# One expert pair leaves the DRAM path: units 4 to 12 instead of 4 to 13 return through accumulating DMAs, unit 13 through one-hot matmuls

## The chip, the cores and the metric

The kernel runs on one core of a Trainium2 chip. The metric is the time of one execution in microseconds (us) as the device gives it; the time before is the median of three runs.

## What is computed

Two transformer blocks follow each other over 512 tokens of width 1024, in float32. Each block is a mixer (attention of one kind beside a recurrence of another), an output projection onto the residual h, and a mixture of experts. The change is in the mixture of the first block:

```python
for e in range(N_EXPERTS):                      # 32 experts, two chosen per token
    h = jax.nn.silu(x2d @ w_gate[e]) * (x2d @ w_up[e])      # 1024 -> 256
    y = y + combine[:, e:e + 1] * (h @ w_down[e])           # 256 -> 1024
h = h + y
```

`combine` is zero but for the two experts that a router chose for the token, so only the rows that an expert has been given are computed. After it comes a norm and the second block.

## The kernel before, in words

**Units.** The 32 experts of the first mixture are worked off in 16 units of two. A unit has 128 lanes, 64 for each expert of the pair; an expert with more than 64 tokens would need a further round, which is a loop over `body` (L1589) whose count is read from memory and is zero for these inputs, so the loop is skipped by a branch on every engine. For each unit u: POOL gathers the rows by an indirect DMA into `xg` (two units ahead), TensorE transposes them (L1609), multiplies with the gate and up weights of both experts (L1711, 64 instructions), ScalarE and VectorE make `hh` (L1714, L1715), TensorE transposes it (L1765, ScalarE copies it to `hT`, L1766), and one unit later the down product is made (L1655, 16 instructions).

**Weights.** Six loads of 1 MB for each unit (gate, up and down of two experts) are issued from SP (L1540) in a fixed order through a ring of buffers: gate and up of u, then down of u - 1, but for the last unit down of 14 first, then gate and up of 15, then its down.

**Return of the rows.** The rows of a unit must be multiplied by their weight and added into the residual h at their tokens. There are two ways.
- One-hot products (`down`, `scatter`): ScalarE and VectorE split the product into a high and a low part (L1785, L1786), VectorE makes a matrix `SC` of ones and zeros from the lanes' token numbers (L1790), and for each of 4 token tiles n and 2 halves d TensorE multiplies `SC` with both parts (L1806, L1807) into a PSUM bank; VectorE adds the bank into `h[:, n]` (L1800). Two banks, `ch` and `pq`, take turns. Units 0 to 3 go this way, two units at a time, and units 14 and 15 together after the skipped loop, in `end`.
- By DRAM (`by_dram`): ScalarE scales the product (L1664), POOL writes its rows by an indirect DMA to a DRAM buffer `yd` (L1665). When the last such unit has written, eight indirect DMAs (L1730), for choice c = 0, 1 and token tile n = 0 to 3, fetch each token's row from `yd` and add it to `h[:, n]` while they write it. A token whose expert isn't among these units has an index out of bounds, and its row is left out. Units 4 to 13 (experts 8 to 27) go this way. `yd` is cleared once, much earlier, in the first mixer (L503).

Which units go by DRAM is set by `FROM` and `BYDRAM` at the top; `far` (L1681) is their range, and the accumulating DMAs stand in the text at `u == far[-1] + 1`, after that step's `by_dram`.

**Order.** Between the engines a framework sets all waits from what the instructions read and write, so a VectorE add into `h[:, n]` waits for the accumulating DMAs into it, and the second accumulate into a tile for the first. The order on each engine is planned ahead from modelled costs: mostly the text's order, but an instruction whose inputs the plan has ready is pulled ahead of one that it has waiting. On the chip each engine then works strictly in that order. All engines pass the skipped loop together. Behind it `end` is written in a fixed order.

Of the kernel before, what the change touches and what calls it, by code (L numbers as in the profile page):

```python
# [25 lines left out]
SILU = "silu_and_others"  # L26

FROM = {1: 8, 2: 0}
BYDRAM = {1: 20, 2: 14}
CAP = {1: 64, 2: 96}  # L30
ZROW = {k: BYDRAM[k] * CAP[k] for k in CAP}
KAPPA = float(np.exp(-0.5))
# [37 lines left out]
def host_consts(inp):  # L70
    pc = {part: np.zeros((128, n), np.float32) for part, n in LAY.n.items()}

    def put(name, a):
        part, o, w = LAY.at[name]
        pc[part][:, o:o + w] = a
# [26 lines left out]
    for k, e in (1, np.arange(32)), (2, np.arange(16)):  # L102
        put("row%d" % k, one * np.where((e >= FROM[k]) & (e < FROM[k] + BYDRAM[k]), CAP[k] * (e - FROM[k]), 1e5))
    put("out1", i[:, None] + 128 * np.arange(16) - CAP[1] * FROM[1])
# [78 lines left out]
class Kern:  # L183
# [1459 lines left out]
    def moe1(self):  # L1643
# [34 lines left out]
        def body(num, wts, idx, first):  # L1678

            ys, prev = [], None  # L1680
            far = range(FROM[1] // 2, (FROM[1] + BYDRAM[1]) // 2) if first else ()  # L1681
            for u in range(2):
# [6 lines left out]
            def down_args(u, hT, num, wts):  # L1689
                return hT, [self.moe_next(mo) for _ in range(2)], wts[:, u:u + 1], onehot(u, yp.tile([128, T], R32, name="SC", bufs=3))  # L1690

            onehot = lambda u, SC: self.onehot(SC, mo, num, u)
            for u in range(mo.U):
# [13 lines left out]
                for m in range(2):  # L1707
                    d = p[:, m * 256:m * 256 + 256]
# [25 lines left out]
                hT = gp.tile([128, 2, 128], F32, name="hT", bufs=1)  # L1734
                turned(hh, hT)
                prev = u, hT
            if not first:
                self.scatter(ys[12:15], 1)
                self.scatter(ys[14:15], 0)
                hT = gp.tile([128, 2, 128], F32, name="hT", bufs=1)  # L1740
                turned(hh, hT)
                return first, None, *down_args(mo.U - 1, hT, num, wts)
# [19 lines left out]
        def turned(hh, hT):  # L1762
            q = self.ps("tr")
            for k in range(2):
                nc.tensor.transpose(q[:, k * 128:(k + 1) * 128], hh[:, k * 128:(k + 1) * 128], self.ident)  # L1765
            nc.scalar.activation(hT, q[:, 0:256].rearrange("p (k t) -> p k t", k=2), AF.Copy)  # L1766

        def end(first, y14, *args):
# [6 lines left out]
            for n in (0, 2, 1, 3):  # L1775
                for d in range(2):
                    self.scatter(ys, d, [n], ("so", "gu", "so", "dn"))

        self.moe_rounds(mo, body, None, end)
        self.sums_two([self.place(mo, 1) for _ in range(NT)], self.place(mo, 1))  # L1780
        mo.cr.close()
# [44 lines left out]
    def moe2(self, out):  # L1826
        nc, tc, mo = self.nc, self.tc, self.mo
        with mo.cx, mo.cr:
# [48 lines left out]
            def body(num, wts, idx, first):  # L1877
# [7 lines left out]
                for u in range(mo.U):  # L1885
# [37 lines left out]
                    if prev and not last:  # L1923
                        y = down(*prev, num, wts, not first or prev[0] >= BYDRAM[2], turned)
                    else:
# [114 lines left out]
```

## Time and profile before

| what | us |
|---|---|
| median of three runs | 1420.56 (1418.53 to 1422.75) |
| the profiled execution's own time | 1419.69 |
| its span, first to last instruction | 1417.9 |
| TensorE busy in the span | 1289.0 (91%) |
| VectorE, ScalarE, POOL busy | 841.6, 701.6, 410.2 |
| moved by DMA | 283.93 MB, mean 200 GB/s |

A span is cut into stretches, and each stretch has its own limit. In a row of the table of stretches the busy times of the engines stand beside the stretch's length, and the DMA share is the mean busy share of the 16 DMA engines. In the timeline a row is the start, the duration, the engine, the line, and what is written from what; "x16" is sixteen instructions in a row, and the bracket is the idle time before and what ended it. The first mixture's last units lie between about 640 and 723 us.

### The profile page before, as it was taken

The page shows a single profiled execution, that of the slowest core. Times are in us where ns is not written, and L with a number is a line of the kernel's source. Part 1 is how long each engine was busy: PE and PEld are TensorE (multiplying, and loading weights), DVE is VectorE, ACT ScalarE, POOL GpSimd, SP SyncE. Part 2 cuts the span into 40 slices and gives each one's busy share as a digit, 9 for nine tenths or more (in the row PEclk, how much of TensorE's full clock was granted, in tenths as well). Part 3 has the DMA queues.
Part 4 walks back from the last instruction along what each step waited for, and adds up shares of the span by engine and source line. Part 5 has one row for each costly group of instructions (what it writes and reads, how often), then busy time and mean ns, then how long its engine had stood idle before and what let it go on. Part 6 is the DMA issues. An engine that isn't in the chain of part 4 may idle for free.

```text
span 1417.9 us, 20482 instructions
## 1 busy us (share of the span) xinstructions
PE 1289.0 (91%) x7792; PEld 927.7 (65%) x7792; DVE 841.6 (59%) x1432; ACT 701.6 (49%) x1217; POOL 410.2 (29%) x329
## 2 busy tenths in 40 slices
PE   7999999999897999999379999999996999999993
PEld 5777766767696555554156776777894666666662
DVE  4679866566656131000075656657637799998895
ACT  6433433334634221211064555555545788888883
POOL 1000224241104101110366102011124555555445
PEclk9999999999998899999789999999997999999996
DMA  5232440000484999999832121202386999889943
GB/s 189 75 89 75 107 109 2 1 1 2 188 330 170 386 419 419 418 418 422 223 101 75 30 76 45 86 24 100 105 334 209 321 360 382 320 332 391 385 166 125
DMA packets 54452, 283.93 MB, mean 200 GB/s; under 512 B 8849, under 2 KB 9745, under 8 KB 28738
## 3 DMA queue, kind: packets, MB, share of 16 engines
q1 hardware_dynamic: 43634, 254.75, 47.9%
q0 software_dynamic: 9840, 26.39, 5.8%
q8 instruction: 66, 1.08, 0.3%
q10 hardware_dynamic: 864, 1.31, 0.3%
q14 instruction: 48, 0.39, 0.1%
HBM read 270.70 MB, written 22.29 MB: 207 GB/s over the span
## 4 chain that ended last, share of the span: by engine, by line
PE 68%; DVE 13%; DMA 11%; ACT 3%; issue 2%; POOL 1%; SPq 0%; DVEq 0%; POOLq 0%; ACTq 0%
PE mm L322 12%; PE ua L1903 4%; PE ua L1901 4%; PE ua L1902 4%; PE mm L1711 4%; DMA ew<-in_e1down_dram 3%; DMA ew<-in_e1up_dram 3%; PE ua L1655 2%; PE sb L322 2%; PE sb L1844 2%; PE sb L1843 2%; PE sb L1845 2%; PE sb L715 2%; DMA ew<-in_e1gate_dram 2%; DVE elo L1625 2%
## 5 line engine op out<-in xcount | busy, mean ns | idle before, releaser
L1625 DVE TENSOR_TENSOR elo<-ew,ehi 128x1024 fp32r<-128x1024 f32 x147 | 231.1, 1614 | 32.9 <-ACT ehi L1624 22.6
L1624 ACT ACTIVATE ehi<-ew 128x1024 fp32r<-128x1024 f32 x192 | 203.0, 1061 | 62.7 <-PE ua L1902 37.2
L322 PE MATMUL mm<-xh,whi 128*128 128x512 f32 (+1 forms) x384 | 155.9, 406 | 4.0 <-DVE hq L1143 3.7
L322 PE MATMUL mm<-xl,whi 128*128 128x512 f32 (+1 forms) x384 | 154.0, 401 | 0.5 <-DVE xl L354 0.3
L322 PE MATMUL mm<-xh,wlo 128*128 128x512 f32 (+1 forms) x384 | 152.8, 398 | 0.0
L1625 POOL TENSOR_TENSOR elo<-ew,ehi 128x1024 fp32r<-128x1024 f32 x45 | 125.9, 2799 | 64.8 <-ACT ehi L1624 63.0
L1711 PE MATMUL mm<-ew,xTh 128*64 128x256 f32 x1024 | 119.2, 386 | 6.4 <-DMA ew<-in_e1up_dram 4.7
L1903 PE MATMUL ua<-elo,xTh 128*96 128x512 f32 x256 | 102.9, 402 | 8.5 <-DVE elo L1625 8.4
L1711 PEld LDWEIGHTS mm<-ew,xTh 128*64 128x64 f32 x1024 | 73.5, 139 | 47.5 <-DMA ew<-in_e1up_dram 6.4
L1715 DVE TENSOR_TENSOR hh<-hh,mm 128x256 f32<-128x256 f32 x16 | 6.7, 421 | 163.5 <-ACT hh L1714 163.5
L1901 PE MATMUL ua<-ehi,xTh 128*96 128x512 f32 x256 | 102.3, 399 | 0.7 <-ACT xTh L1613 0.6
L1902 PE MATMUL ua<-ehi,xTl 128*96 128x512 f32 x256 | 101.8, 398 | 0.0
L296 ACT ACTIVATE whi<-w 128x1024 fp32r<-128x1024 f32 x53 | 55.9, 1057 | 91.1 <-PE mm L322 72.5
L297 DVE TENSOR_TENSOR wlo<-w,whi 128x1024 fp32r<-128x1024 f32 x52 | 63.7, 1227 | 51.7 <-ACT whi L296 51.5
L1596 POOL DMA_INDIRECT xg<-xd,idx x32 | 36.7, 1147 | 196.2 <-PE sb L1609 123.7
L322 PEld LDWEIGHTS mm<-xh,whi 128*128 128x128 f32 x384 | 73.4, 191 | 23.2 <-DVE hq L1143 5.4
L322 PEld LDWEIGHTS mm<-xl,whi 128*128 128x128 f32 x384 | 73.7, 192 | 16.7 <-issue 3.5
L322 PEld LDWEIGHTS mm<-xh,wlo 128*128 128x128 f32 x384 | 73.6, 192 | 16.0 <-issue 2.2
L1655 PE MATMUL ua<-ew,hT 128*64 128x512 f32 x240 | 66.4, 600 | 1.2 <-ACT hT L1766 1.1
L1714 ACT ACTIVATE hh<-mm 128x256 f32<-128x256 f32 x16 | 6.1, 383 | 112.8 <-PE mm L1711 112.8
L1903 PEld LDWEIGHTS ua<-elo,xTh 128*96 128x96 f32 x256 | 41.9, 164 | 30.6 <-DVE elo L1625 11.2
L1167 POOL TENSOR_TENSOR hAT<-hAT,hmt 128x512 f32<-128x512 f32 x16 | 22.1, 1381 | 118.9 <-DVE hmt L1166 118.3
(640 smaller groups left out, 3028.0 us busy)
## 6 DMA issues: line engine op xcount, KB each, us to landing
ew<-in_e1up_dram SPq DMA_DIRECT2D x32, 1024.0 KB, 17.8
ew<-in_e2up_dram SPq DMA_DIRECT2D x32, 1024.0 KB, 8.3
ew<-in_e2gate_dram SPq DMA_DIRECT2D x32, 1024.0 KB, 9.2
ew<-in_e2down_dram SPq DMA_DIRECT2D x32, 1024.0 KB, 12.5
ew<-in_e1gate_dram SPq DMA_DIRECT2D x31, 1024.0 KB, 19.5
ew<-in_e1down_dram SPq DMA_DIRECT2D x30, 1024.0 KB, 20.6
w<-in_win_dram SPq DMA_DIRECT2D x53, 512.0 KB, 3.6
ew<-in_wout_dram SPq DMA_DIRECT2D x8, 1024.0 KB, 6.9
```

The costliest lines, as they stand in the source:

```text
L296: nc.scalar.activation(hi, s, AF.Copy)
L297: (eng or nc.vector).tensor_tensor(lo, s, hi, OP.subtract)
L322: mm = lambda w, x, start=False, stop=False: nc.tensor.matmul(p[:, s], w[:, k], x[:, k, s], start=start, stop=stop, skip_group_check=parts ...
L715: nc.tensor.matmul(po[d, 0:128], v[:, kb, d], wT[hh][:, kb * 128:(kb + 1) * 128], start=kb == 0, stop=kb == b)
L1596: return self.nc.gpsimd.indirect_dma_start(out=xg, out_offset=None, in_=mo.xd, in_offset=bass.IndirectOffsetOnAxis(ap=idx[:, u:u + 1], axi ...
L1624: self.hi = nc.scalar.activation(hi, s, AF.Copy)
L1625: self.lo = (nc.gpsimd if pool else nc.vector).tensor_tensor(lo, s, hi, OP.subtract)
L1655: nc.tensor.matmul(p[hs(a)], hT[:, k, hs(a)], w[a][:, k * 1024 + d * 512:k * 1024 + d * 512 + 512], start=k == 0, stop=k == 1)
L1711: nc.tensor.matmul(d[hs(a)], xT[:, k, hs(a)], w[2 * m + a][:, k * 256:k * 256 + 256], start=k == 0, stop=k == KD - 1)
L1901: nc.tensor.matmul(p, xh[:, kk], hi[:, s], start=kk == 0, stop=False)
L1902: nc.tensor.matmul(p, xl[:, kk], hi[:, s], start=False, stop=False)
L1903: nc.tensor.matmul(p, xh[:, kk], lo[:, s], start=False, stop=kk == KD - 1)
```

## The change

`BYDRAM[1]`, the number of experts that return by DRAM, goes from 20 to 18. So `far` is units 4 to 12, the eight accumulating DMAs are issued at u = 13, unit 13 takes the branch of `down` (one-hot matrix, high and low part) at u = 14, and `yd`, its clearing and the bounds shrink from 1280 to 1152 rows. After the loop over the units, when unit 15's gate and up products have been written down in the text and before its transpose, unit 13's rows are added by `scatter`, half 0 for all four tiles, then half 1.

```diff
-BYDRAM = {1: 20, 2: 14}
+BYDRAM = {1: 18, 2: 14}
...
                 hT = gp.tile([128, 2, 128], F32, name="hT", bufs=1)
                 turned(hh, hT)
                 prev = u, hT
-            if not first:
+            if first:
+                for d in range(2):
+                    self.scatter(ys[far[0]:], d)
+            else:
                 self.scatter(ys[12:15], 1)
                 self.scatter(ys[14:15], 0)
                 hT = gp.tile([128, 2, 128], F32, name="hT", bufs=1)
```

`ys` holds one entry for each unit that came back through `down` so far: units 0 to 3, and now unit 13 as its fifth.

## Rows read from the trace of the kernel before

**Rows 1.** Table of stretches: length, busy PE, PEld, DVE, ACT, POOL, clock, DMA share, GB/s.
```profile
668.00:683.70 15.70, 12.86 (x64) 5.82 (x64) 1.99 (x4) 3.40 (x6) 0.97 (x2) 1.00 0.97 404
...
691.50:708.60 17.10, 0.00 (x0) 0.00 (x0) 0.00 (x0) 0.00 (x0) 6.21 (x4) 0.56 0.71 120
...
668.00:705.80 37.80, 17.82 (x102) 8.50 (x100) 2.41 (x5) 4.17 (x8) 13.53 (x9) 0.84 0.91 270
```

**Rows 2.** Chain of waits, 600 to 740 us: start, us, what.
```profile
687.53 19.46 DMA h<-yd,row
707.00 1.62 issue
708.62 6.25 PE ua L1655 x16
```

**Rows 3.** Timeline of POOL, 500 to 720 us: start, us, what.
```profile
659.23 0.97 POOL L1665 DMA_INDIRECT yd<-ot,out  x1 [15.23 <-ACT hT L1766]
675.07 0.97 POOL L1665 DMA_INDIRECT yd<-ot,out  x1 [14.87 <-ACT hT L1766]
683.70 1.63 POOL L1730 DMA_INDIRECT h<-yd,row  x1 [7.65 <-DMA yd<-ot,out]
...
698.78 1.55 POOL L1730 DMA_INDIRECT h<-yd,row  x1 [0.31 <-issue]
```

**Rows 4.** The loop's line, ns min/median/max, first mixture, then second; VectorE's last work.
```profile
L1589 POOLq EVENT_SEMAPHORE  x16: 17/43/43, 705.8 to 708.5; - x16
...
L1589 DVEq COMPARE_BRANCH  x3: 41/51/61, 690.9 to 708.2; - x3
...
L1589 PEldq COMPARE_BRANCH  x3: 100/190/5383, 691.7 to 708.4; - x3
...
L1589 PEldq COMPARE_BRANCH  x3: 82/187/3444, 1396.9 to 1410.9; - x3
...
1404.75 0.75 DVE L1823 SCALAR_TENSOR_TENSOR ew<-h,bss,ew 128x512 f32<-128x512 f32 x1 [0.19 <-ACT bss L1820]
```

**Rows 5.** DMA queues 668 to 683 us, then 683 to 708: packets, MB, share.
```profile
q1 hardware_dynamic: 812, 5.84, 93.4%
q0 software_dynamic: 144, 0.25, 4.4%
...
q0 software_dynamic: 1152, 2.58, 64.0%
```

**Rows 6.** DMA queues in the 2 us from 664, from 688 and from 692.
```profile
q1 hardware_dynamic: 96, 0.68, 80.5%
q0 software_dynamic: 90, 0.19, 24.1%
...
q1 hardware_dynamic: 22, 0.10, 12.8%
...
q1 hardware_dynamic: 8, 0.03, 3.7%
```

**Rows 7.** Timelines: TensorE from 676 us, VectorE from 650 us.
```profile
680.88 3.67 PE L1711 MATMUL mm<-ew,xTh 128*64 128x256 f32 x32 [1.68 <-DMA ew<-in_e1gate_dram]
685.99 3.67 PE L1711 MATMUL mm<-ew,xTh 128*64 128x256 f32 x30 [1.43 <-DMA ew<-in_e1up_dram]
690.58 0.44 PE L1765 MATMUL sb<-pc_c,hh 128*128 128x128 f32 x2 [0.93 <-DVE hh L1715]
...
657.43 0.88 DVE L1790 TENSOR_SCALAR ew<-io,num 128x512 fp32r<-128x512 f32 x2 [4.39 <-PE ua L1655]
...
678.69 0.75 DVE L1786 SCALAR_TENSOR_TENSOR ew<-ua,wts,ew 128x512 fp32r<-128x512 f32 x1 [9.47 <-ACT ew L1785]
```

**Rows 8.** Timeline of VectorE, adds of units 0 and 1.
```profile
507.96 0.69 DVE L1800 TENSOR_TENSOR h<-h,ch 128x512 f32<-128x512 f32 x1 [1.08 <-PE ch L1807]
508.88 0.69 DVE L1800 TENSOR_TENSOR h<-h,pq 128x512 f32<-128x512 f32 x1 [0.23 <-PE pq L1807]
```

**Rows 9.** DMA issues, 162 to 192 us: KB each, us to landing.
```profile
yd<-qz SPq DMA_DIRECT2D x1, 5120.0 KB, 28.3
```

## The prediction

> **What bounds the kernel now.** I read the table of stretches first, because the page's 91% busy TensorE is a mean over stages with different limits. In the first mixture the DMA engines set the pace: their share is 0.97 from 668 to 683.7 us, while TensorE is busy for 12.86 of the 15.7 [rows 1]. Then comes a hole: from 691.5 to 708.6 TensorE, VectorE and ScalarE do nothing, and the DMA share is 0.71 [rows 1]. The chain of waits says what the hole is. It runs over the accumulating transfers from DRAM into h (from 687.53 to 707.0) and 1.62 us of issue, and TensorE starts unit 15's down product at 708.62 [rows 2]. The timeline of POOL gives the order: unit 13's row write is issued at 675.07, the first of the eight accumulates at 683.70, the last at 698.78; unit 12's write had been issued at 659.23 [rows 3]. The rows of the loop line show the end: POOL's first wait on the loop's line that passes is at 705.8, 7.0 us after it issued the last accumulate, and TensorE's branch out of the skipped loop is at 708.4 [rows 3, 4]. So from the last landing (call it L) to TensorE's restart it is 708.62 - 705.8 = 2.8 us. All engines pass this loop, and nothing after it starts before; a shift of the restart passes on to the end one to one.
>
> **The change, part by part.**
>
> *The accumulates start a unit earlier.* They wait for the last row write, now unit 12's: issued at 659.23 and not 675.07, so 15.8 us earlier [rows 3]. With no contention L would be 690.0. But there is contention: the first accumulate would come at 659.23 + (683.70 - 675.07) = 667.9, into a stretch whose DMA share is 0.97 [rows 1]. The accumulates are dear: the software queue had 64.0% of 25 us, 16.0 us of all 16 engines for 2.58 MB, where the hardware queue moves 5.84 MB in 93.4% of 15 us [rows 5]. So I count engine time. Between 668 and 705.8 the share is 0.91 of 37.8 us: 34.4 us of work, 3.4 us idle [rows 1]. Taken out of it: unit 13's row write, 4.4% of 15 us = 0.66 us [rows 5], and the two experts of 20 that no longer return this way, a tenth of 16.0, 1.6 us. Work left: 32.1 us. If some engine was never idle, L moves by -2.3; if the idle time is all regained, by -5.7. For the first speaks that the weight queue still has 12.8% of the engines at 688 and 3.7% at 692, one or two engines that lag [rows 6], and a transfer lands with its slowest engine. I take -3.3, nearer to the lagging end: L = 702.5. The ends for the range are -15.8 and 0 (work only leaves).
>
> *What is late next: unit 15's weights.* Its up product starts at 685.99 for want of its weights and the transpose behind it is over at 691.0 [rows 7], 14.8 us ahead of L. The accumulates share the engines with these weights now. While a row write met them, 90 of its packets went beside 96 of theirs [rows 6], so turns are about even. A packet is 0.64 x 25 x 16 / 1152 = 0.22 us of an engine for the accumulates and 0.934 x 15 x 16 / 812 = 0.28 for weights [rows 5]: the weights keep 0.55 of the time. From the accumulates' first data at about 670 to the up weights at 686 they have some 14 us of work (93.4% of the time); at 0.55 it takes 25.5: up15 comes at about 696 and not 686, and its product and transpose (5.0 us, 685.99 to 691.02) end at 701.0, before L. The sum doesn't need them.
>
> *Unit 13 by one-hot products: its making.* One one-hot (0.44 us on VectorE), two 0.75 us subtractions on VectorE, two copies on ScalarE in place of two others, no row write on POOL [rows 7]. VectorE is busy 1.99 of 15.7 us there, and TensorE 12.86 and waiting for weights [rows 1]: nothing. Without that cover it would be 1.9 us.
>
> *Unit 13 by one-hot products: its adding.* Eight pairs of matmuls and eight adds of 0.69 us into h. The list holds units 0 to 3 and then 13, so the slice is unit 13 alone. An add into h[:, n] must wait for both accumulates of tile n. The order is half 0 for all tiles, then half 1, so after L there remain the add of tile 3, half 0, and all four of half 1. Adds with two banks in turn follow each other at about 0.93 us with four matmuls each [rows 8]; with two matmuls each, about 0.8. So 0.8 + 4 x 0.8 = 4.0 us after L; TensorE is through with its last pair 0.9 us earlier. Bounds: 0.7 (only one add left) and 4.7. Queued behind the waiting adds on VectorE is only the loop; on TensorE, by the text's order, the same (rival B is the other order).
>
> *The loop is entered late.* Before, VectorE and TensorE came to its branch at 690.9 and 691.7 and had 15 us to spare; TensorE's branch alone took 5.38 us in that time [rows 4]. Now both come last. The second mixture shows the price of coming late: VectorE's last work ends at 1404.75 + 0.75 = 1405.5, and TensorE's branch out is at 1410.9 [rows 4]: 5.4 us, and 0.2 us to the next matmul. That takes the place of the 2.8 us. Bounds: 2.8, and TensorE's path: last pair 3.1 after L, 0.3 to the branch, 5.4, and the 1.6 of issue [rows 2, 4] make 10.4 after L, 0.8 more than the sum below.
> The Trainium skill (Runtime: NRT & Kernel Launch, Instruction fetch mechanics) says that a taken branch to a target outside the current window makes the engine fetch the page by DMA before it goes on. TensorE's two long branches (5.38 and 3.44 us) agree; VectorE's own record is 0.05 us and shows no such stall, so by that record alone the entry would stay near 2.8 us, and the result is rival D.
>
> *Zero rows.* The clearing of the DRAM rows, 5120 KB in 28.3 us from 162 us on [rows 9], shrinks by a tenth. In the waits of that stretch (155 to 215 us) no engine waits for a transfer: nothing.
>
> **Sum.** Restart = L + 4.0 + 5.6 = L + 9.6, before L + 2.8; L moves by -3.3: -3.3 + 6.8 = **+3.5 us**. The profiled execution has 1419.69 (span 1417.9 and 1.8 around it); 1423.2 by that, and since the median of the runs is 0.9 above it, 1424.1. What a measurement can tell from no change is 0.3%, 4.3 us: this is inside it, on the slow side.
>
> **Rivals.**
> B, slower: the adding stands ahead of unit 15's gate and up products in TensorE's queue. The planner does pull later work forward: the one-hot of unit 15 runs on VectorE at 657.43 beside unit 14's, 23 us before the up product behind which it stands in the text [rows 7]. A pair of unit 13 whose bank is still held by an add that waits for L would then block gate (3.67 us) and up with its transpose (5.0 us): restart = L + 3.1 + 8.7 + 5.6 = L + 17.4, 7.8 more than the sum: +11.3, 1431.9. If only up is behind it, 4.1 more, +7.6, 1428.2. It decides from the third pair on, the first that needs a bank back. Against it: the planner has to think the accumulates land before those weights, which were issued earlier.
> C, faster: the accumulates run beside the weights without taking time from them. L = 690.0, adds until 694.0, restart 699.6, 9.0 earlier: 1411.6. It begins where L moves by -11.1 and the restart by -4.3: 1416.3. Against it: both shares add up to 104.6% and not more [rows 6].
> The Trainium skill (DMA: Bandwidth & Descriptors, Issuing engines are not separate DMA queues) says that transfers of all issuers run on the same 16 engines and interleave; by that rule C can't be whole, and the trace's sum of shares agrees.
> D, nothing: the entry is as cheap as before (2.8), and the adds cost 1.5 to 4.0 after L: -3.3 + 1.5 = -1.8 to +0.7, some 1420.
> That the change doesn't do what it says I exclude by the list above.
>
> **How the numbers follow.** Chances: forecast 0.55, B 0.17, C 0.16, D 0.12. The forecast's own range, from L by -5.7 to -2.3 and the entry's 0.8, is 1421.5 to 1426.5; 0.40 of its 0.55 lie within 0.3%, 0.15 above. Slower: 0.15 + 0.17 = 0.32. Same: 0.40 + 0.12 = 0.52. Faster: 0.16. Of C the range leaves out the lower two thirds (0.10), of B what lies at its full price or above (0.10): 1415 to 1431.
>
> **What would show it.** Right: the first accumulate at about 668, the DMA share near 1.0 until about 702; unit 15's up product at 690 or later and not at 686; five of unit 13's adds after the last landing; TensorE's branch of 3 us or more with no cover, restart near 712. Wrong: the restart before 705 (C), or unit 13's pairs ahead of unit 15's gate and up with TensorE idle between them (B).

## The result and the profile after

The changed kernel takes 1436.92 us (median of 4 runs, 1435.25 to 1440.99); the kernel before, on the same chip, 1420.92. The ratio is 1.0114 (95% interval 1.0095 to 1.0133): 16 us slower, above the forecast of 1424.1 and above its range. It went the way of rival B, and further than B's price.

All of it comes from the hole at the end of the first mixture. The timeline of TensorE of the changed kernel (start, length, line, operation, and in brackets the idle time before it and what ended it):

```profile
675.47 0.50 PE L1809 MATMUL ch<-oh,SC 128*128 128x512 f32 x1
...
676.59 1.93 PE L1655 MATMUL ua<-ew,hT 128*64 128x512 f32 x4
698.01 0.80 PE L1809 MATMUL ch<-oh,SC 128*128 128x512 f32 x1 [19.48 <-DVE h L1803]
...
703.07 0.80 PE L1809 MATMUL ch<-oh,SC 128*128 128x512 f32 x1 [0.19 <-DVE h L1803]
703.80 4.58 PE L1655 MATMUL ua<-ew,hT 128*64 128x512 f32 x12
...
711.50 7.12 PE L1711 MATMUL mm<-ew,xTh 128*64 128x256 f32 x62
719.55 0.44 PE L1768 MATMUL sb<-pc_c,hh 128*128 128x128 f32 x2 [0.93 <-DVE hh L1715]
728.73 5.76 PE L1655 MATMUL ua<-ew,ew 128*64 128x512 f32 x16 [8.74 <-issue]
```

L1809 and L1810 are the pairs that add unit 13. The first two pairs stand at 675.47, ahead of unit 14's down product (L1655 into ua), of which four matmuls get through. Then TensorE stands for 19.48 us: its next pair needs a PSUM bank back, and the add that frees it waits for an accumulate. Twelve of the sixteen down matmuls and all 64 of unit 15's gate and up products (L1711) run only behind the last landing, with everything they read long there. In the kernel before they were done by 691 [rows 7]. VectorE's timeline shows what the pairs waited for:

```profile
697.26 0.69 DVE L1803 TENSOR_TENSOR h<-h,ch 128x512 f32<-128x512 f32 x1 [20.21 <-DMA h<-yd,row]
700.92 0.69 DVE L1803 TENSOR_TENSOR h<-h,pq 128x512 f32<-128x512 f32 x1 [2.97 <-DMA h<-yd,row]
702.33 0.69 DVE L1803 TENSOR_TENSOR h<-h,ch 128x512 f32<-128x512 f32 x1 [0.73 <-DMA h<-yd,row]
703.68 0.69 DVE L1803 TENSOR_TENSOR h<-h,pq 128x512 f32<-128x512 f32 x1 [0.66 <-DMA h<-yd,row]
...
719.07 0.42 DVE L1715 TENSOR_TENSOR hh<-hh,mm 128x256 f32<-128x256 f32 x1 [6.78 <-ACT hh L1714]
```

Four adds, one for each tile of half 0, each released by an accumulate; the other four follow the products. The table of stretches, the stretches chosen as in [rows 1] (length, busy PE, PEld, DVE, ACT, POOL, clock, DMA share, GB/s):

```profile
668.00:683.70 15.70, 9.84 (x38) 3.49 (x34) 1.92 (x3) 2.03 (x4) 7.90 (x5) 0.94 1.03 379
676.60:698.00 21.40, 1.92 (x5) 0.45 (x4) 1.14 (x2) 0.00 (x0) 7.94 (x6) 0.62 0.97 276
704.70:728.70 24.00, 14.02 (x85) 6.99 (x81) 4.40 (x7) 2.14 (x4) 0.00 (x0) 0.86 0.13 47
```

The hole of 17.1 us in [rows 1] is now one of 21.4 with TensorE at 1.92 us of work, and behind it 24.0 us in which TensorE does for 14.02 us mostly what it used to do under the transfers, while the DMA engines are all but empty (0.13). The clock fell to 1.2 GHz while TensorE stood (0.50 in every stretch from 690 to 705.7), as it did in the hole before.

The accumulates did move. POOL's timeline, against [rows 3]:

```profile
662.31 0.98 POOL L1665 DMA_INDIRECT yd<-ot,out  x1 [17.38 <-ACT hT L1769]
671.38 1.63 POOL L1730 DMA_INDIRECT h<-yd,row  x1 [8.09 <-DMA yd<-ot,out]
...
693.26 1.55 POOL L1730 DMA_INDIRECT h<-yd,row  x1 [2.44 <-DMA h<-yd,row]
```

The first is issued at 671.38 in place of 683.70, the last at 693.26 in place of 698.78. The queues in the 2 us from 688 (packets, MB, share of the 16 engines):

```profile
q1 hardware_dynamic: 70, 0.42, 51.5%
q0 software_dynamic: 99, 0.18, 46.8%
```

And the loop's line, POOL's mark behind the last landing and TensorE's branches, against [rows 4] (count, ns min/median/max, first and last start):

```profile
L1589 PEldq COMPARE_BRANCH  x3: 100/292/3269, 720.3 to 728.4; - x3
L1589 POOLq INC_SWDGE_SEM  x1: 907/907/907, 703.8 to 703.8; - x1
```

That mark stood at 706.1 before, so the last landing, which I put 0.3 us ahead of the mark as before (705.8 and 706.1), came 2.3 us earlier, at 703.5. From there to the restart it was 2.8 us; now it is 728.73 - 703.5 = 25.2. The restart is 20.1 us late, the end of the program 16.2. Most of the difference is a spell of half clock that the kernel before has some 70 us after its restart and the changed one doesn't. The two rows are of the kernel before and, 20 us later, of the changed one; the clock is third from the end:

```profile
776.00:788.00 12.00, 9.06 (x28) 6.96 (x27) 8.17 (x14) 5.73 (x11) 0.00 (x0) 0.72 0.29 87
```

```profile
796.00:808.00 12.00, 9.04 (x42) 6.56 (x42) 9.95 (x17) 7.11 (x13) 0.00 (x0) 1.00 0.30 87
```

There 2.8 of the 3.9 us are given back: the same instructions stand 19.8 us later ahead of that spell and 17.0 behind it.

### The profile page after: what moved, and what is told of

Same layout as the page of the kernel before. It is cut to its first block, busy times and chain, and to the rows that moved or that the text cites. A ratio compares the mean times of both kernels' runs of the same rounds, so it can differ in the third digit from the quotient of the medians.

```text
span 1434.1 us, 20540 instructions
## 1 busy us (share of the span) xinstructions
PE 1292.3 (90%) x7808; PEld 929.2 (65%) x7808; DVE 850.0 (59%) x1443; ACT 700.7 (49%) x1217; POOL 409.8 (29%) x328
## 5 line engine op out<-in xcount | busy, mean ns | idle before, releaser
L1711 PE MATMUL mm<-ew,xTh 128*64 128x256 f32 x1024 | 119.2, 386 | 2.5 <-DMA ew<-in_e1up_dram 1.9
L1711 PEld LDWEIGHTS mm<-ew,xTh 128*64 128x64 f32 x1024 | 74.0, 139 | 43.1 <-issue 4.7
L1655 PE MATMUL ua<-ew,hT 128*64 128x512 f32 x240 | 68.9, 609 | 1.2 <-DMA ew<-in_e1down_dram 1.2
## 6 DMA issues: line engine op xcount, KB each, us to landing
ew<-in_e1gate_dram SPq DMA_DIRECT2D x31, 1024.0 KB, 19.8
```

The source lines that it names most:

```text
L1655: nc.tensor.matmul(p[hs(a)], hT[:, k, hs(a)], w[a][:, k * 1024 + d * 512:k * 1024 + d * 512 + 512], start=k == 0, stop=k == 1)
L1711: nc.tensor.matmul(d[hs(a)], xT[:, k, hs(a)], w[2 * m + a][:, k * 256:k * 256 + 256], start=k == 0, stop=k == KD - 1)
```

## The experiments

Theory 1: the order in TensorE's queue. Theory 2: the accumulates slow unit 15's weights, and TensorE would have been late anyway. Theory 3: the skipped loop costs TensorE 8 to 9 us from whenever it gets there. All ratios are to the kernel before, run on the same chip beside them.

**1. The adding behind unit 15's products.**

```diff
+                            up = nc.tensor.matmul(d[hs(a)], xT[:, k, hs(a)], ...
+                hid = nc.vector.tensor_tensor(hh, hh, p[:, 256:512], OP.mult)
...
+                with tc.issue_after(up.ins), tc.issue_after(hid.ins):
                     for d in range(2):
                         self.scatter(ys[far[0]:], d)
```

> The changed kernel with unit 13's adding put behind unit 15's last up product in TensorE's queue and behind unit 15's product of gate and up in VectorE's; all else as changed. Theory 1 (the order: 12 matmuls of unit 14's down product and all of unit 15's gate and up stood behind an adding that waited for the accumulates): the last accumulate lands near 703.6 us again, TensorE is through with unit 15 near 694 and only the adds and the loop's entry stand behind the landing, restart 10 to 11 us after it, near 714 instead of 728.7, and 1423 to 1427 us in all. Theory 2 (the accumulates' turns on the queues slow unit 15's weights, and TensorE would have been late whatever the order): unit 15's products still end near 718 and the time stays at 1434 to 1437.

Measured: 1424.87 us (10 runs), ratio 1.0013 (1.0003 to 1.0024). TensorE's timeline:

```profile
692.44 3.67 PE L1711 MATMUL mm<-ew,xTh 128*64 128x256 f32 x30 [1.83 <-DMA ew<-in_e1up_dram]
...
701.08 0.50 PE L1810 MATMUL pq<-oh,SC 128*128 128x512 f32 x1 [2.71 <-DVE h L1804]
...
707.79 0.63 PE L1811 MATMUL pq<-oh,SC 128*128 128x512 f32 x1
716.69 6.57 PE L1655 MATMUL ua<-ew,ew 128*64 128x512 f32 x16 [8.27 <-POOL ew L402]
```

The up product ends at 696, under the transfers; restart 716.69. Two orders by `issue_after` take back 12 of the 16 us: theory 1 holds. Of theory 2 the first half holds (the up product starts at 692.44, at 685.99 before), but it doesn't make TensorE late, and that half falls. That the time is the one forecast for this order is luck: the restart is 12.4 us behind the last landing (its mark at 704.6) and not 9.6, which is 8.1 us later than before, where the forecast had 3.5. The profiled execution ends 6.3 us later than that of the kernel before (spans 1424.2 and 1417.9), and the medians differ by 3.0.

**2. Unit 13 added after the loop,** with units 14 and 15, its tiles in two slots of the weights' ring.

```diff
+                elif prev and far and prev[0] > far[-1]:
+                    y13 = down(prev[1], ..., onehot(u - 1, self.place(mo, 0, R32)[:, 0:T]), self.place(mo, 0, R32)...)
...
-            if first:
-                for d in range(2):
-                    self.scatter(ys[far[0]:], d)
-            else:
+            if not first:
...
-            return first, y14, hT, w, wt, SC
+            return first, [y13, y14], hT, w, wt, SC
...
-            ys = ([y14] if first else []) + [down(*args)]
+            ys = (y14 if first else []) + [down(*args)]
```

> The changed kernel with unit 13's one-hot products not added before the loop but after it, with those of units 14 and 15 (8 more pairs of matmuls there). Theory 1 (order) and theory 3 (TensorE pays 8 to 9 us at the loop when it comes to it last): TensorE enters the loop near 695 and waits there for nothing but the last accumulate at 703 to 704; restart 2 to 3 us behind it, near 706; the 8 pairs cost 8 x 0.46 = 3.7 us after the restart: 1419 to 1425 us. If the loop's entry costs 8 us behind the last landing as well (rival), restart near 712 and 1426 to 1430 us.

Measured: 1414.73 us, ratio 0.9955 (0.9938 to 0.9971): faster than both kernels. TensorE's timeline:

```profile
690.54 3.67 PE L1711 MATMUL mm<-ew,xTh 128*64 128x256 f32 x30 [1.79 <-DMA ew<-in_e1up_dram]
695.13 0.44 PE L1769 MATMUL sb<-pc_c,hh 128*128 128x128 f32 x2 [0.93 <-DVE hh L1715]
703.95 5.20 PE L1655 MATMUL ua<-ew,ew 128*64 128x512 f32 x16 [8.38 <-issue]
```

TensorE is in the loop by 696 and waits there for the landing (mark at 701.5); restart 2.7 us behind it. The eight pairs cost less than the 3.7 us expected: from the restart to the next stage's first VectorE work (L354) it is 729.63 - 703.95 = 25.7 us, and 24.1 in experiment 3, which has no such pairs. 1.6 us, then.

**3. Unit 13's adding left out;** its one-hot and its down product stay.

```diff
-            if first:
-                for d in range(2):
-                    self.scatter(ys[far[0]:], d)
-            else:
+            if not first:
```

> The changed kernel with unit 13's adding left out (its one-hot table and its down product stay): the earlier accumulates alone. If the adding is the whole loss, restart near 706 (last landing near 703.6 and 2.8 us more), so 2 us under the kernel before: 1416 to 1421 us. If the earlier accumulates themselves cost by contention, 1424 us or more.

Measured: 1416.52 us, ratio 0.9961 (0.9947 to 0.9975). Restart 705.85. The whole loss is in the adding; what is left of the change, the earlier accumulates and the missing row write, gains.

**4. The kernel before without its accumulates.**

```diff
-                if far and u == far[-1] + 1:
-                    for c in range(2):
-                        for n in range(NT):
-                            nc.gpsimd.indirect_dma_start(out=self.h[:, n], ..., compute_op=OP.add)
```

> The kernel before with the eight accumulating DMAs left out (units 4 to 13 are not added): what the accumulates cost it in all, and TensorE's entry into the loop alone. TensorE came to the loop at 691.7 us. If its entry by itself takes 8 to 9 us (as behind the changed kernel's adding), restart near 700 and 1411 to 1414 us; if it is cheap (2.8 us, as the time from the last landing to the restart), restart near 695 and 1405 to 1408 us.

Measured: 1408.26 us, ratio 0.9908 (0.9891 to 0.9924). TensorE's branches, and its restart:

```profile
L1589 PEldq COMPARE_BRANCH  x3: 100/192/3664, 693.1 to 698.5; - x3
...
698.74 6.06 PE L1655 MATMUL ua<-ew,ew 128*64 128x512 f32 x16 [5.95 <-issue]
```

Restart at 698.74, 5.6 us behind the first branch: between the two expectations, and the number that the prediction took from the second mixture. So entering late costs 5.6 here and 8.4 in the changed kernel (720.3 to 728.7).

**5. As 1, tile by tile over four banks.**

```diff
-                    for d in range(2):
-                        self.scatter(ys[far[0]:], d)
+                    for n in range(NT):
+                        for d in range(2):
+                            self.scatter(ys[far[0]:], d, [n], ("so", "gu", "so", "dn"))
```

> As the first experiment (unit 13's adding behind unit 15's last up product), but tile by tile over four PSUM banks instead of half by half over two: the first six adds wait for no more than the accumulates of the first three tiles, and TensorE's last pair needs a bank that is free some 2 us before the last landing. In the first experiment TensorE reached the loop at 708.0 us, 3.6 us behind the last landing (704.4), and restarted 8.7 us after that. Theory 3 (the loop's entry costs TensorE 8 to 9 us from whenever it gets there): TensorE is there near 703, restart near 711 to 712, so 5 us less than the first experiment: 1418 to 1421 us. Rival (the entry waits for VectorE's last add, which comes out about the same): restart near 715, 1423 to 1425 us.

Measured: 1417.03 us (10 runs), ratio 0.9974 (0.9964 to 0.9984). TensorE, VectorE's last add, and POOL's wait for a gain vector:

```profile
700.54 0.40 PE L1812 MATMUL pq<-oh,SC 128*128 128x512 f32 x1
...
709.06 6.42 PE L1655 MATMUL ua<-ew,ew 128*64 128x512 f32 x16 [7.91 <-issue]
...
704.92 0.68 DVE L1805 TENSOR_TENSOR h<-h,ua 128x512 f32<-128x512 f32 x1
...
711.40 2.35 POOL L402 TENSOR_TENSOR ew<-ew 128x1024 f32<-128x1024 f32 x1 [6.13 <-DMA ew<-in_attn_g_dram]
```

TensorE is at the branch at 701.0 and restarts 8.1 us later, with the landing (mark at 704.5) as in experiment 1. So it is TensorE's arrival that sets the restart here, as theory 3 has it, and neither the landing nor VectorE's last add. With another order of the eight adds, and four banks for them, the change is faster than the kernel before.

**6, 9 and 11. Was the early start the gain?** Three tries to give experiment 2 the late accumulates of the kernel before. The first moved their place in the text by a unit, the second put them in the last unit, behind unit 14's rows in the text, the third made POOL wait for data:

```diff
-                if far and u == far[-1] + 1:
+                if far and u == far[-1] + 2:
...
+                    with tc.issue_after(self.last.ins):
                         for c in range(2):
...
+                    gate = nc.gpsimd.tensor_copy(gp.tile([128, 1], F32, name="gate"), y14[1][1][1][:, 0:1])
+                    with tc.issue_after(gate.ins):
                         for c in range(2):
```

> As the second experiment (unit 13 added after the loop), with the accumulates issued one unit later, where the kernel before has them. If that kernel's gain (7 us under the kernel before) comes from the early accumulates, the last one lands near 705 instead of 701.3, restart near 707.7 instead of 704, and the time is 1417 to 1420 us. If it comes from elsewhere (unit 13's write and its turns on the queue gone), it stays at 1413 to 1416 us.

Measured: 1414.31 us, ratio 0.9953 (0.9936 to 0.9970). The first accumulate went out at 668.06, as in experiment 2 (667.97): the text's place doesn't hold it back. This repeats experiment 2 and tells nothing of the start.

> As the second experiment (unit 13 added after the loop), with the eight accumulates held until unit 14's rows are computed (some 681 us in place of 668): the kernel before has them from 683.7. The last experiment of this kind moved only their place in the text, and their issue stayed at 668, so it repeated the second one. If the last landing is set by how much the DMA engines have to move in all (they are busy without a break from 668 to 697), it stays at 701 to 704 us, restart 704 to 706, 1413 to 1417 us. If it is set by when the accumulates start, the last landing comes at 706 to 711, and 1418 to 1424 us.

Measured: 1416.42 us, ratio 0.9969 (0.9958 to 0.9980). First accumulate at 671.94, mark at 703.8. The instruction that the order names (`self.last`) is ScalarE's, and the accumulates, which POOL issues, went out some 10 us before unit 14's rows were there; a miss again.

> As the second experiment (unit 13 added after the loop), with a one-column copy of unit 14's rows on GpSimd ahead of the eight accumulates, so that the first of them can't be issued before some 681 us (the last two experiments of this kind, which moved the issue in the text or in the planner's order alone, left it at 668 and 672). If the last landing is set by all that the DMA engines have to move (less by unit 13's write than in the kernel before), it stays where the second experiment had it, 701 to 704 us, restart 704 to 707, 1413 to 1417 us. If the early start was the gain, the last landing goes back to 705 to 708 as in the kernel before, restart 708 to 711, 1418 to 1422 us.

Measured: 1418.96 us (11 runs), ratio 0.9981 (0.9972 to 0.9990). POOL's timeline:

```profile
682.39 0.18 POOL L1702 COPY gate<-ew 128x1 f32<-128x1 f32 x1 [18.93 <-DVE ew L1791]
683.13 1.65 POOL L1706 DMA_INDIRECT h<-yd,row  x1 [0.56 <-issue]
...
698.87 1.55 POOL L1706 DMA_INDIRECT h<-yd,row  x1 [0.30 <-issue]
```

Now the start is that of the kernel before, and the mark too: 706.1, restart 708.47. The early start is worth 2.9 to 4.6 us at the mark (703.2 in experiment 6, 701.5 in experiment 2) and 4 in the time, for a start 15 us earlier. That the total work of the DMA engines sets the landing, as the prediction had it, is refuted at this size: this kernel has the changed kernel's smaller work, and its landing is that of the kernel before. The 2.8 us between the medians lie elsewhere, since the restart is the same (708.47, 708.62 before); the two profiled executions end only 0.6 us apart (spans 1417.3 and 1417.9), so the traces don't show where.

**7. The adding behind unit 14's down product only** (dn14 is its last matmul).

```diff
+                with tc.issue_after(dn14.ins):
                     for d in range(2):
                         self.scatter(ys[far[0]:], d)
```

> The changed kernel with unit 13's adding behind unit 14's last down product in TensorE's queue, still ahead of unit 15's gate and up. Theory 1 by its parts: of what stood behind the adding in the changed kernel, the down product (4.6 us) is out and about half of the 64 gate and up products (9.4 us for all) stays in: restart 717 to 722 us, between the first experiment's 716.7 and the changed kernel's 728.7, 1425 to 1431 us in all. If the order counts only in what waits for the last landing (rival), no more than the first experiment: 1423 to 1426 us.

Measured: 1434.97 us, ratio 1.0099 (1.0079 to 1.0119), above what I expected. TensorE:

```profile
703.23 5.62 PE L1712 MATMUL mm<-ew,xTh 128*64 128x256 f32 x32
...
709.90 3.67 PE L1712 MATMUL mm<-ew,xTh 128*64 128x256 f32 x30
...
723.80 5.56 PE L1655 MATMUL ua<-ew,ew 128*64 128x512 f32 x16 [8.86 <-issue]
```

Not half but all of gate and up came behind the waiting pairs, and the first 32 ran mostly at half clock (0.65 granted from 703.2 to 708.9). Restart 22.6 us behind the landing (its mark at 701.5) against 25.2: the down product alone is the small part.

**8. The change without the accumulates.** The edit of experiment 4 on the changed kernel; the adding stays where the change has it.

> The changed kernel with the eight accumulating DMAs left out (units 4 to 12 are not added), unit 13's adding where the change has it, ahead of unit 14's down product and unit 15's gate and up in TensorE's queue. If the order costs only because the adds wait for the accumulates, TensorE runs through the adding and reaches the loop near 692; restart 5.5 to 9 us later, 697 to 701, so 1407 to 1413 us. If the adding itself or its place costs more than that, 1416 us or more.

Measured: 1410.56 us, ratio 0.9925 (0.9908 to 0.9943). Pairs, down product, gate and up run through with no stop over 0.4 us between 675.55 and 694.4; restart 704.77, later than expected, since TensorE reached the loop at 696.1 and not 692. The same order costs little when the adds have nothing to wait for: against experiment 4, which has neither the change nor the accumulates, the restart is 6.0 us later and the median 2.3, within the two intervals. It is the wait for the accumulates, handed on through the banks, that costs most of the 16 us.

**10. As 2, without the accumulates** (the edit of experiment 4 on experiment 2).

> As the second experiment, with the eight accumulating DMAs left out (units 4 to 12 are not added): TensorE's entry into the loop alone, with no adding of unit 13 ahead of it. In the kernel before without accumulates it took 5.6 us from the branch to the first matmul, in the changed kernel without them 8.7 us (a second stop of 3.1 us inside). If the second stop belongs to the adding ahead of the loop, the entry takes 5.6 us here and the restart comes near 698 to 699, 1407 to 1411 us in all; if not, 8.7 us, restart near 701 to 702, 1410 to 1414 us.

Measured: 1406.88 us, ratio 0.9903 (0.9885 to 0.9921). Branches 690.9 to 695.9, restart 696.14: 5.2 us. The longer entry goes with the adding ahead of the loop, and theory 3's 8 to 9 us hold only there.

The entries side by side, from the first branch on the loop's line to the first matmul behind it:

| kernel | adding ahead of the loop | branch | first stop, us | second stop, us | restart | entry |
|---|---|---|---|---|---|---|
| changed | yes | 720.3 | 3.3 | 3.1 | 728.73 | 8.4 |
| experiment 1 | yes | 708.0 | 3.7 | 2.8 | 716.69 | 8.7 |
| experiment 5 | yes | 701.0 | 3.5 | 2.1 | 709.06 | 8.1 |
| experiment 7 | yes | 715.3 | 3.8 | 2.7 | 723.80 | 8.5 |
| experiment 8 | yes | 696.1 | 3.6 | 3.1 | 704.77 | 8.7 |
| experiment 4 | no | 693.1 | 3.7 | none | 698.74 | 5.6 |
| experiment 10 | no | 690.9 | 3.3 | none | 696.14 | 5.2 |

## Why the prediction was wrong

The step that failed is the place of the adding: "Queued behind the waiting adds on VectorE is only the loop; on TensorE, by the text's order, the same (rival B is the other order)." It took the order of the text for TensorE's order, and gave the other one 0.17. The planner had the other one: the restart came 25.2 us behind the last landing and not 9.6, and 12.4 once the text's order was held (experiment 1). Point by point:

- *The order.* The planner put the first pairs ahead of unit 14's down product and of unit 15's gate and up. The rows had shown it pulling later work forward [rows 7]; the argument against B (that it would have to think the accumulates land early) was a guess on the planner's estimates that no row carried. Experiment 1 isolates the step: with the text's order the loss shrinks from 16 us to 3. Why the planner chose so wasn't tried.
- *The time with the text's order.* 1424.87 against the forecast 1424.1, but not by the forecast's terms: the restart was 8.1 us late and not 3.5. That "a shift of the restart passes on to the end one to one" failed too, by 3.9 us in the changed kernel (20.1 and 16.2).
- *B's price.* It had the restart 17.4 us behind the landing; measured 25.2. Gate, up and transpose were right (8.7 expected; 711.50 to 719.99 is 8.5). The adds and pairs ahead of them had 3.1 and took 8.0 (703.5 to 711.5), because twelve of unit 14's down matmuls were among them (4.58 us), which B had not put behind the adding. The entry had 5.6 and took 8.7.
- *The loop's entry.* Entering late does cost: 5.6 and 5.2 us in experiments 4 and 10, without the adding, 8.1 to 8.7 with it. That TensorE comes last and pays is right; the size was 3 us off. The Trainium skill (Runtime: NRT & Kernel Launch, Instruction fetch mechanics) says that a taken branch out of the fetched window stalls the engine until the target page is there. The first stops in the table agree, at 3.3 to 3.8 us; rival D, which had no such stall, is refuted. But that the prediction's 5.6 meets experiment 4 is luck. In the second mixture TensorE came to the branch at 1396.9 [rows 4], not late, and its stop of 3.44 us was over by 1401.8. What it waited for last, until 1409.9, was SyncE, which came last to its branch and was through at 1409.9 (the loop's line of SyncE; the last two numbers are the first and the last start):

```profile
L1589 SPq EVENT_SEMAPHORE  x20: 17/28/28, 1409.9 to 1413.8; - x20
L1589 SPq COMPARE_BRANCH  x3: 33/38/43, 1406.0 to 1413.9; - x3
```

- *The last landing.* 2.3 us earlier, -3.3 expected. In the eight kernels that start early and have the accumulates the mark moved by -1.5 (experiment 1) to -4.6 (experiments 2 and 7), so the expected number lies inside that spread, and the range of -5.7 to -2.3 leaves out experiments 1 and 5. Its working failed: it counted what the DMA engines have to move, and experiment 11 moves as little, from the old start, and lands when the kernel before does. The share named for it, near 1.0 until about 702, was 0.87 from 696 to 698 and 0.40 from 698 to 700. Unit 12's write was 3.1 us late in the changed kernel (662.31, 659.23 before), which no run explains.
- *Contention.* In the 2 us from 688 the share of the weights' queue fell to 51.5% beside 46.8% for the accumulates: even turns, as said, and their sum leaves no room for rival C. The Trainium skill (DMA: Bandwidth & Descriptors, Issuing engines are not separate DMA queues) has the transfers of all issuers on the same 16 engines, and the trace agrees. But unit 15's up product comes at 690.54 in experiment 2, later than 685.99 [rows 7] by 4.6 us and not by 10. The queues of experiment 2 from 670 to 690.5:

```profile
q1 hardware_dynamic: 777, 5.52, 65.6%
q0 software_dynamic: 708, 1.42, 36.3%
```

The weights kept 0.656 of the engines and not 0.55: the prediction's 14 us of work take 21.3 at that, to 691.3. The turns are even while both queues have work, and the accumulates hadn't always: the fifth and those behind it waited on POOL for earlier landings and went out 3.8 to 4.4 us apart.

- *The adds behind the landing.* 4.0 us expected for five; in experiment 1 the last of five ends at 709.14 (708.45 + 0.69), 4.8 behind the landing (704.3).
- *Making unit 13.* Nothing, as said, as far as the runs show: experiment 3 has it and is faster than the kernel before; no run has it alone.
- *The range.* The forecast's own range was put at 1421.5 to 1426.5; its terms (L by -5.7 to -2.3, and 0.8) give 1421.7 to 1425.9.

## What to carry to other kernels

A vector add that waits for a transfer also holds the PSUM bank it reads, and so every matmul that stands behind the next user of that bank: before such an add is placed, count what TensorE has in its queue behind it, and where a planner writes that queue, fix the order with a dependency rather than trust the text. A wait that can't be avoided belongs behind the last product or, better, behind the next point where the engines wait anyway: after the loop the same eight pairs cost 1.6 us. And an engine that used to reach a skipped loop early hides what entering it costs; whoever makes it come last has to price that entry, from a run in which nothing covers it.

## What the runs showed of the hardware

TensorE's way out of a skipped loop has one stop of 3.3 to 3.8 us at its second branch, and in five of the seven kernels of the table a second one of 2.1 to 3.1. The second always stood between the eighth and the ninth of the 12 waits that follow that branch, and always ended 6.9 to 7.6 us after that branch began, whatever came in between. The chain of waits of the changed kernel lays it at a transfer that SyncE issued just before:

```profile
721.42 4.96 DMA ew<-in_attn_g_dram
726.37 2.35 issue
728.73 5.76 PE ua L1655 x16
```

Experiment 5 says otherwise: TensorE restarts there at 709.06, while POOL still waits for that same transfer until 711.40. Nor is it another wait: in all five the semaphores that the ninth wait names had been reached before the stop began (in the changed kernel at 720.6, the stop is from 724.8 to 728.0). What ends inside both stops is a packet of 16 KB of the queue that the profile calls instruction. The queues during the second stop of the changed kernel, 724.9 to 727.9:

```profile
q1 hardware_dynamic: 79, 0.26, 21.2%
q8 instruction: 1, 0.02, 2.0%
```

In all seven kernels the first stop ends 1.4 to 1.6 us after such a packet has ended, and in the five the second ends 1.3 to 1.5 us after the next one (in the changed kernel the packets end at 722.45 and 726.65, the stops at 723.91 and 727.95). So both stops go with a fetch of instructions and not with data. Why the next packet stops nothing in experiments 4 and 10, where it comes as well (at 697.83 and 695.23), stays open.

VectorE, ScalarE, GpSimd and SyncE show branches of 0.03 to 0.07 us on the same line, but such a record doesn't mean that there is no stop. In the second mixture of the kernel before they stand 3.4 to 4.4 us between a branch and the next wait, and what VectorE, ScalarE and GpSimd wait for there had come by 1404.7. VectorE's branch is at 1405.8; its waits between 1407 and 1411 begin at 1410.2:

```profile
L1589 DVEq EVENT_SEMAPHORE  x9: 49/50/50, 1410.2 to 1410.9; - x9
```

So the prediction's reading that VectorE shows no such stall [rows 4] holds for the record only.

Accumulates that start 15 us earlier (experiments 2 and 6 against 11) land 2.9 to 4.6 us earlier. The DMA share is 0.94 or more in every 4 us from 668 to 696 in experiment 2, so most of the head start seems to go into sharing the engines with the weights, which is argued from that share and not shown.
